# A hybrid attention and state-space layer: some inputs laid out by the host, and steps moved among groups, gates, turn and root

## The chip, the cores and the metric

The kernel runs on one core of a Trainium2 chip. The metric is the device time of one execution, in microseconds (us), as the median of several runs. The engines are named as in the profile: PE is TensorE (matmul; PEld is its weight load), DVE is VectorE, ACT is ScalarE, POOL is GpSimd, SP is SyncE, whose queue carries nearly all DMA issues of this kernel. PSUM is the memory that matmuls write; the kernel uses it in eight banks of 128 x 512 words.

## The reference, cut to what matters

One decoder layer with batch 1, sequence 1024 and model width 1024, all in fp32:

```python
c_act = silu(c)
shift, scale, gate = split(c_act @ w_ada + b_ada, 3)          # w_ada: 1024 x 3072
h = rms_norm(x, norm_in_gain) * (1 + scale) + shift
q, k, v, z_attn, xbc, dt_raw, z_ssm = split(h @ w_in)         # 4 x 1024, 1536, 16, 1024 columns
o = stick_breaking_attention(q, k, v)                         # 16 heads of 64
y_attn = rms_norm(o, sb_norm_gain) * silu(z_attn)
xs, B, C = split(silu(causal_depthwise_conv(xbc, conv_w, conv_b)))
dt = softplus(dt_raw + dt_bias); a = -exp(a_log)
y = ssd_scan(xs, dt, a, B, C, d_skip)                         # Mamba-2, 16 heads, chunks of 128
y_ssm = rms_norm(y * silu(z_ssm), ssm_norm_gain)
x = x + gate * (concat(y_attn, y_ssm) @ w_out)
out = rms_norm(x, norm_f_gain)
```

Stick-breaking attention weights key s for query t with sigmoid(z_ts) times the product of (1 - sigmoid(z_tj)) over the keys j between s and t.

## The kernel before

Projections run as fp32r matmuls of 512 columns in three terms: each operand is split into a high part (rounded to fp32r) and a low part (the rest), and high x high, low x high and high x low are summed in one PSUM bank. `hh[k]`, `hl[k]` are the two parts of the modulated and normalised x, features on partitions (k = 0..7, 128 features each) and 1024 tokens along the row; `whi`, `wlo` are those of a weight tile. A split costs a copy and a subtraction, on DVE and ACT.

The program has three stages. In the first and the third the order of every engine's instructions is that of the code (`pinned[0]` is true, and `K` or the `Engine` wrapper pins each instruction; that is why most DVE, ACT and SP instructions have line 62, the wrapper's, in the profile). In the second a scheduler orders them.

1. *Start.* `c` and other vectors are loaded as rows and turned into columns (`cols`) by a PE transpose (L125). x comes in eight tiles `xt[i]` of 128 tokens (named `big`), `w_ada`'s shift and scale columns in four quarters `c_` of 256 + 256 columns (`load_ada`, two DMAs for each of four tiles, rows of 1 KB). `norm_sq` squares a tile on ACT with a sum along the row, `norm_rt` makes the root on ACT and the reciprocal on DVE, `norm_by` scales the tile on DVE. `turn_x` transposes four 128 x 128 blocks on PE into a bank of `pt` or `pv` (L522); `h_full` modulates from there (scale `gsc`, shift `shc`) into `hh[k]` and a full copy (`hfs`, named `be`), and `h_low` subtracts for `hl[k]`. The first 512 tokens are `hb` = 0, the others `hb` = 1. `mm_h(k, hb)` is 12 matmuls (L562): the first four column tiles of `xbc`, summed over k in four `pz` banks. `fillers` (L582) are matmuls without a use of their own. After this `late_consts` makes columns of the convolution's and the norms' vectors, with two more transposes (L160, L163).
2. *State-space stage*, in the scheduler's order: the other `xbc` tiles, `dt`, the first values of attention, the convolutions, and two groups (`ssd_group`) of eight chunks, with gates (`gate_ssm`) and the first pair's q and k beside the second.
3. *Attention and output*, in the order of the code. Heads go in eight pairs p. `ROUND` lists a pair's steps: `scores` of a group of query blocks (L1028), `turned` (transposes of the weights and ACT's copies), `values` (L1120, into the one `pv` bank). Beside them run side jobs, a list for each pair (`SIDES`): gates, q and k, v, and at p = 6 the turn. `side_step` issues the next piece of a job, mostly three matmuls (L304 for features by tokens); `tick` moves a modelled clock, by which `after(t, f)` issues DMAs and splits later. A finished projection bank (`pj`, two of them) is emptied by ACT: the evacuations `evac` in `gate_ssm`, `qk` and `zgate` run a nonlinear pass (or the rounding copy) from the bank, then copy it to an `hf` tile with `emptied`, from which DVE goes on. `rows_s` is the root of the state-space output's sums of squares, within `inproj_v` (L350). `scores` has one rule on side work:

```python
        while side_left() and not 0.6 < left[0] < 3.6:
            side_step()
```

That is: before a group of scores the side job is moved to a place in a bank's sum where no evacuation is due (`left[0]` is what remains of it in us). `turn` is the last gate projection, with `hl` used up for good: it sums the terms with `hl` and `whi` first for both token halves, then loads `w_out`'s lower half into the freed `hl` tiles (`load_half`, tiles `wor`, one DMA for each 128 rows), and splits it while the other terms run. Then comes the output projection (`out_ssm`, L1163) and the tail with the final norm.

The profile's names: `pz`, `pj`, `pt`, `pv` are banks; `th`, `om`, `be`, `bc`, `bs`, `raw`, `st`, `sq`, `v`, `hf` are pools of tiles in SBUF. The functions that the change touches:

Of the kernel before, what the change touches and what calls it, by code (L numbers as in the profile page):

```python
# [26 lines left out]
def hybrid_layer_kernel(  # L27
# [3 lines left out]
    c: bass.AP,  # L31
    w_ada: bass.AP,
    b_ada: bass.AP,
    norm_in_gain: bass.AP,
    w_in: bass.AP,
    conv_w: bass.AP,
    conv_b: bass.AP,
    dt_bias: bass.AP,
    a_log: bass.AP,
    d_skip: bass.AP,  # L40
    sb_norm_gain: bass.AP,
    ssm_norm_gain: bass.AP,
# [81 lines left out]
    pr = bank(pv, "pv")  # L124
    K(T.transpose(pr[:, :32], rows[0:32, :], ident[0:32, 0:32]))  # L125
    cols = const("cols", [P, P])
    V.tensor_copy(cols[:, 0:32], pr[:, :32])
    cact = const("cact", [P, 8])
# [1419 lines left out]
```

## Time and profile before

| what | value |
|---|---|
| time, median of 3 runs | 1049.31 us (1048.99 to 1051.03) |
| time of the profiled execution | 1048.86 us |
| its span | 1047.1 us |
| PE busy | 1031.9 us, 99% |
| DVE busy | 766.5 us, 73% |
| ACT busy | 547.8 us, 52% |
| granted TensorE clock, mean | 0.999 |
| DMA | 96.17 MB, mean 92 GB/s |

The span runs from the first to the last instruction that the profiler recorded. A PE record of a matmul is longer than the distance to the next one, since matmuls are pipelined, so a PE that shows 99% can still have room within its instructions; the distance from one start to the next is the measure of what a matmul costs. In the rows of groups and of the timeline the fields are start (in a timeline), duration, engine, line, operation, output <- inputs, shape, type and count; what stands in brackets is idle time of the engine just before, and what ended it. In the rows of windows the first number is the window's length, then come PE, PEld, DVE, ACT and POOL with their busy time and count, the granted clock, the DMA engines' busy share (in us) and GB/s.

### The profile page before, as it was taken

Reading aid. Unit: us, or ns where it says so; the run is one execution under the profiler, and the core shown is the slowest. Engines: PE = TensorE matmul, PEld = TensorE weight load, DVE = VectorE, ACT = ScalarE, POOL = GpSimd, SP = SyncE. Lnnn points to the kernel's source line nnn. Section 1 sums busy time; section 2 is a strip of 40 time slices with the busy share of each in tenths; the row PEclk is TensorE's granted clock in tenths of the full one; section 3 lists DMA queues with packets and bytes.
Section 4 is the critical chain, followed back from the end, with each engine's and each line's share of the span. In section 5 each row is a group of like instructions: output and inputs, shape, how many; then the busy total and the mean of one; then the engine's idle time right before and its main releaser. Section 6 shows DMA issues by size and latency. Waiting matters only on the chain.

```text
span 1047.1 us, 16416 instructions
## 1 busy us (share of the span) xinstructions
PE 1031.9 (99%) x6365; PEld 847.2 (81%) x6365; DVE 766.5 (73%) x1339; ACT 547.8 (52%) x1218; POOL 2.7 (0%) x23
## 2 busy tenths in 40 slices
PE   7999999999999999999999999999999999999997
PEld 5789888777888887898887888878977778788886
DVE  5738879998838884764897668987578879755554
ACT  4755497767415564564554556555457556521111
POOL 0000000000000000000000000000000000000000
PEclk9999999999999999999999999999999999999999
DMA  9610333233302221111221102311120522665432
GB/s 349 238 42 22 84 105 106 71 102 101 101 21 61 81 81 30 56 27 41 81 71 41 51 21 81 81 42 41 32 63 29 202 101 71 214 221 172 148 114 78
DMA packets 91562, 96.17 MB, mean 92 GB/s; under 512 B 5998, under 2 KB 75994, under 8 KB 91484
## 3 DMA queue, kind: packets, MB, share of 16 engines
q1 hardware_dynamic: 88828, 86.45, 26.1%
q10 hardware_dynamic: 2656, 8.67, 2.6%
q8 instruction: 50, 0.82, 0.3%
q14 instruction: 28, 0.23, 0.1%
HBM read 78.26 MB, written 16.84 MB: 91 GB/s over the span
## 4 chain that ended last, share of the span: by engine, by line
PE 93%; DVE 2%; ACT 2%; DMA 2%; issue 0%; SPq 0%; DVEq 0%; ACTq 0%
PE pj L304 40%; PE pj L1163 16%; PE pv L1120 6%; PE pt L1093 3%; PE pz L562 3%; PE pj L350 3%; PE pj L354 3%; PE pj L351 3%; PE pz L1093 3%; PE pj L1028 2%; PE pz L1028 2%; PE pt L1028 2%; PE pz L824 1%; PE pv L838 1%; PE pz L829 1%; PE pj L1497 1%
## 5 line engine op out<-in xcount | busy, mean ns | idle before, releaser
L304 PE MATMUL pj<-hh,whi 128*128 128x512 f32 x544 | 220.2, 405 | 0.0
L304 PE MATMUL pj<-hh,wlo 128*128 128x512 f32 x544 | 214.0, 393 | 0.0
L304 PE MATMUL pj<-hl,whi 128*128 128x512 f32 x544 | 212.5, 391 | 0.0
L304 PEld LDWEIGHTS pj<-hh,whi 128*128 128x128 f32 x544 | 102.2, 188 | 23.9 <-issue 5.5
L304 PEld LDWEIGHTS pj<-hh,wlo 128*128 128x128 f32 x544 | 102.1, 188 | 22.6 <-issue 0.7
L304 PEld LDWEIGHTS pj<-hl,whi 128*128 128x128 f32 x544 | 102.4, 188 | 19.9 <-issue 1.0
L62 DVE TENSOR_TENSOR wlo<-raw,whi 128x512 fp32r<-128x512 f32 (+1 forms) x109 | 75.3, 692 | 23.5 <-ACT whi L62 16.6
L62 DVE TENSOR_TENSOR_SCAN om<-om 128x896 f32<-128x896 f32 (+2 forms) x48 | 87.3, 1818 | 1.7
L62 ACT COPY be<-pt 128x512 f32<-128x512 f32 (+1 forms) x80 | 38.6, 503 | 64.6 <-PE pt L1093 63.9
L350 PE MATMUL pj<-whi,hh 128*128 128x256 f32 (+1 forms) x224 | 65.1, 291 | 0.5 <-ACT v L62 0.5
L354 PE MATMUL pj<-whi,hl 128*128 128x256 f32 (+1 forms) x224 | 64.4, 288 | 0.0
L351 PE MATMUL pj<-wlo,hh 128*128 128x256 f32 (+1 forms) x224 | 63.6, 284 | 0.0
L1028 PE MATMUL pz<-big,big 64*128 64x256 f32 (+2 forms) x432 | 59.7, 334 | 0.0
L62 DVE TENSOR_TENSOR be<-be,om 128x767 f32<-128x767 f32 (+2 forms) x64 | 56.9, 889 | 3.1 <-DVE be L62 0.4
L62 ACT ACTIVATE be<-pz 128x127 f32<-128x127 f32 (+4 forms) x112 | 58.6, 529 | 0.0
L62 DVE TENSOR_TENSOR_SCAN bc<-bc 128x128 f32<-128x128 f32 (+2 forms) x64 | 56.6, 885 | 2.2
L304 PE MATMUL pj<-hh,st 128*128 128x512 f32 x160 | 56.1, 400 | 0.0
L1120 PE MATMUL pv<-be,v 128*64 128x256 f32 (+1 forms) x512 | 53.7, 362 | 0.0
L62 ACT ACTIVATE be<-be,acum 128x128 f32<-128x128 f32 x128 | 39.5, 390 | 24.5 <-DMA be<-acT_d 19.3
L1120 PEld LDWEIGHTS pv<-be,v 128*64 128x64 f32 x512 | 34.8, 137 | 20.1 <-issue 4.7
L62 DVE CAST whi<-raw 128x512 fp32r<-128x512 f32 x75 | 31.3, 418 | 23.2 <-PE pj L354 16.0
L62 ACT ACTIVATE th<-v 128x1024 f32<-128x1024 f32 (+2 forms) x9 | 8.5, 944 | 73.7 <-DVE v L62 73.7
(301 smaller groups left out, 2321.0 us busy)
## 6 DMA issues: line engine op xcount, KB each, us to landing
raw<-in_w_in_dram SPq DMA_DIRECT2D x98, 256.0 KB, 2.8
be<-acT_d ACTq DMA_DIRECT2D x16, 512.0 KB, 4.0
big<-in_x_dram SPq DMA_DIRECT2D x10, 512.0 KB, 6.5
aw<-in_w_ada_dram SPq DMA_DIRECT2D x16, 256.0 KB, 5.8
u_d<-big SPq DMA_DIRECT2D x8, 512.0 KB, 2.6
y_d<-bc SPq DMA_DIRECT2D x8, 512.0 KB, 2.6
raw<-in_w_ada_dram SPq DMA_DIRECT2D x16, 256.0 KB, 2.6
raw<-u_d SPq DMA_DIRECT2D x16, 256.0 KB, 2.9
```

What stands on the lines that cost most here:

```text
L62: return lambda *args, **kw: K(op(*args, **kw))
L304: K(T.matmul(ps, w[:, ws], h[:, b * HALF:(b + 1) * HALF], start=(k == 0 and n == 0), stop=(k == KT - 1 and n == 2)))
L350: K(T.matmul(ps[:, :n], h_hi[k][:, ts_], whi[:, ws], start=(k == 0), stop=False))
L351: K(T.matmul(ps[:, :n], h_hi[k][:, ts_], wlo[:, ws], start=False, stop=False))
L354: K(T.matmul(ps[:, :n], h_lo[k][:, ts_], whi[:, ws], start=False, stop=(k == KT - 1)))
L562: K(T.matmul(acc[f][:, c0:c1], w[:, f * P:(f + 1) * P], h[:, sl], start=(k == 0 and n == 0 and c0 == 0), stop=(k == KT - 1 and n == 2)))
L824: K(T.matmul(po, xd[:, 0, h, :], m[:, h, :], start=True, stop=(ch == 0)))
L829: K(T.matmul(po, st[:, h, :], abc[:, h, :], start=False, stop=True))
L1028: K(T.matmul(zs[b, e][:, y0:y0 + mw], a[r, i * P:(i + 1) * P], k_[r, m0:m0 + mw], start=(n == 0), stop=(n == 2)))
L1093: K(T.transpose(from_[:, (j - j0) * P:(j - j0 + 1) * P], be[:, j * P:(j + 1) * P], ident))
L1120: K(T.matmul(ps[64 * e:64 * e + 64, (q0 + u) * P:(q0 + 2) * P], vs[p][:, j * P + 64 * e:j * P + 64 * e + 64], tl[e][:, u:2, x0 + j * P:x0 ...
L1163: K(T.matmul(ps, y[:, ks], w(k, b), start=(k == 0 and n == 0), stop=(k == KT - 1 and n == 2)))
```

## The change

*Inputs.* The host hands over, beside x as it is, `x_t` (the second 512 tokens of x with features first, eight tiles of 128 x 512), `w_mod` (`w_ada`'s shift and scale columns as four quarters of four tiles 128 x 1024 that lie in one piece), `w_gate` and `b_gate` (the gate's columns), and `vecs` (the vectors as 148 columns). The row loads, the three transposes and the copies behind them go; `cols` is loaded in two DMAs, 32 columns first and 116 late. `load_ada` is one DMA a tile, 4 KB rows. The tile `xt[4]` is loaded ahead of the last quarter of `w_ada`, and `xt[5]` to `xt[7]` alternate with the last two weight tiles; `x_t` comes behind them.

*Second half of x.* `xt[4]` to `xt[7]` are read for their sums of squares alone: tiles 4 to 6 on ACT earlier than before, tile 7 on DVE. `scales` makes the reciprocals and multiplies the identity by them (four diagonals in an `hf` tile); four fp32 matmuls of ones by diagonals, between the two halves of `mm_h(6, 0)`, spread 1/rms of 512 tokens over all partitions in the `pv` bank. `second(k)` multiplies `x_t[k]` by that row on DVE, from PSUM and in place, and modulates the product as before, both passes on ACT and from SBUF. The 32 transposes of this half are gone.

*Groups, gates, turn, root.* The rule on side work is now a function, `to_window`, that `values` calls too, for pairs 0 to 6, once the next pair's q and k exist. In the pinned stage the gates' and `qk`'s evacuations copy the bank first and run the pass from the copy. `turn` orders its first matmuls so that `hl[0]` to `hl[3]` are free before the last six of the sixteen, and loads each pair of `w_out`'s blocks by one DMA as a tile comes free. The square root and reciprocal of `rows_s` wait in `quiet` for the next `turned` step of query block 2.

```diff
-    rows = mk(sp, "cbm", [P, 2, P], bufs=2)[:, 0, :]
-    A.dma_start(rows[0:8, :], c.rearrange("o (k p) -> (o k) p", p=P))
-    A.dma_start(rows[8:24, :], b_ada[:, 0:2048].rearrange("o (k p) -> (o k) p", p=P))
-    A.dma_start(rows[24:32, :], norm_in_gain.rearrange("o (k p) -> (o k) p", p=P))
+    cols = const("cols", [P, 192])
+    A.dma_start(cols[:, 0:32], vecs[:, 0:32])
...
-    pr = bank(pv, "pv")
-    K(T.transpose(pr[:, :32], rows[0:32, :], ident[0:32, 0:32]))
-    V.tensor_copy(cols[:, 0:32], pr[:, :32])
...
-            for e in range(2):
-                SP.dma_start(t_[:, :, e, :],
-                             w_ada[0][2 * n * P:2 * (n + 1) * P, e * D + c_ * 256:e * D + (c_ + 1) * 256]
-                             .rearrange("(k p) f -> p k f", p=P))
+            SP.dma_start(t_, w_mod[c_, n])
...
+    load_x(4)
     load_ada(3)
-    load_w4(6), load_w4(7)
-    for i in range(4, TB):
-        load_x(i)
-    late_loads()
+    load_x(5), load_w4(6), load_x(6), load_w4(7), load_x(7)
...
+    def by_rstd(k):
+        V.tensor_tensor(x_turned[k], x_turned[k], scale_of["row"], op=ALU.mult)
+    def scales(is_):
+        if not scale_of:
+            scale_of["diag"] = mk(sp, "hf", [P, HALF], bufs=2)
+        V.reciprocal(rstd[:, is_[0]:is_[-1] + 1], rstd[:, is_[0]:is_[-1] + 1])
+        for i in is_:
+            V.tensor_scalar_mul(scale_of["diag"][:, (i - 4) * P:(i - 3) * P], ident, rstd[:, i:i + 1])
+    def second(k):
+        by_rstd(k)
+        modulate(k, 1, x_turned[k])
...
+    load_xt()
+    late_loads()
+    V.scalar_tensor_tensor(junk, xt[7], 1.0, xt[7], op0=ALU.mult, op1=ALU.mult, accum_out=ssq[:, 7:8])
+    scales((4, 5, 6))
+    h_full(6, 0, pts[0])
+    h_low(6, 0)
+    norm_root(7)
+    scales((7,))
+    h_full(7, 0, pts[1])
+    split_lo(7)
+    h_low(7, 0)
+    mm_h(6, 0, (0, 1))
+    scale_of["row"] = bank(pv, "pv")
+    for i in range(4):
+        K(T.matmul(scale_of["row"][:, i * P:(i + 1) * P], ones, scale_of["diag"][:, i * P:(i + 1) * P],
+                   start=True, stop=True))
+    mm_h(6, 0, (2, 3))
+    second(0)
     mm_h(7, 0, (0, 1))
-    modulate(0, 1, full_v=True)
-    norm_by(6, 256), norm_by(7, 256)
+    second(1)
     mm_h(7, 0, (2, 3))
...
     for k in range(1, KT):
         if k + 2 < KT:
-            modulate(k + 2, 1)
+            second(k + 2)
         mm_h(k, 1)
...
-            A.activation(zg, ps, AF.Sigmoid)
-            V.scalar_tensor_tensor(zg, zg, cols[:, 92 + p:93 + p], emptied(ps), op0=ALU.mult, op1=ALU.mult)
+            full = emptied(ps)
+            A.activation(zg, full, AF.Sigmoid)
+            V.scalar_tensor_tensor(zg, zg, cols[:, 92 + p:93 + p], full, op0=ALU.mult, op1=ALU.mult)
...
+    def to_window():
+        while side_left() and not 0.6 < left[0] < 3.6:
+            side_step()
...
     def values(p, i_):
         while side_left() and clock[0] < free_at[0]:
             side_step()
+        if p < 7:
+            while p + 1 not in box:
+                side_step()
+            to_window()
...
-        for g, b in ((0, 0), (1, 0), (0, 1), (1, 1)):
-            for q in range(4):
+        for b, qs in ((0, (0, 1, 2, 3, 4, 5)), (1, (0, 1, 2, 3)), (0, (6, 7)), (1, (4, 5, 6, 7))):
+            for q in qs:
...
+                if b and q < 4:
+                    load_pair(0, q, hp.tile([P, 2, HALF], F32, tag=f"hl{q}", name=f"wor{q}"))
...
-            if (g, b) == (0, 1):
-                load_half(0, lambda q: hp.tile([P, 2, HALF], F32, tag=f"hl{q}", name=f"wor{q}"))
...
-        A.activation(r, r, AF.Sqrt, scale=1.0 / D, bias=eps_t[:, 1:2])
-        V.reciprocal(r, r)
+        def factors():
+            A.activation(r, r, AF.Sqrt, scale=1.0 / D, bias=eps_t[:, 1:2])
+            V.reciprocal(r, r)
+        quiet.append(factors)
...
             elif what == "t":
+                if i == 2 and quiet:
+                    quiet.pop()()
                 turned(p + before, i)
```

Instructions move on several engines. On DVE, at the entry to the second half of x, there stood before (`big` are the x tiles, `rstd` the reciprocals, `be` <- `raw`,`sq` the low part of a weight tile):

```order
L62 RECIPROCAL rstd<-rstd 128x1 x2
L62 TENSOR_SCALAR big_182<-big_182,rstd 128x1024
L62 TENSOR_SCALAR big_184<-big_184,rstd 128x1024
L62 TENSOR_TENSOR be_427<-raw_180,sq_495 128x512
L62 TENSOR_TENSOR hl_528<-be_203,hh_527 128x512
L62 TENSOR_TENSOR hl_532<-be_203,hh_531 128x512
L62 RECIPROCAL rstd<-rstd 128x1 x2
L62 TENSOR_SCALAR big_186<-big_186,rstd 128x256
L62 TENSOR_SCALAR big_188<-big_188,rstd 128x256
L62 TENSOR_SCALAR be_203<-pv_574,gsc,shc 128x512
L62 TENSOR_TENSOR hl_264<-be_203,hh_263 128x512
```

and now, in the same place (`hf` are the diagonals, `bc` the tiles of `x_t`, `pv_533` the row of scales):

```order
L56 SCALAR_TENSOR_TENSOR om_506,cols<-big_164 128x1024
L56 RECIPROCAL rstd<-rstd 128x3
L56 TENSOR_SCALAR hf_508<-ident,rstd 128x128 x3
L56 TENSOR_TENSOR hl_514<-be_168,hh_513 128x512
L56 RECIPROCAL rstd<-rstd 128x1
L56 TENSOR_SCALAR hf_508<-ident,rstd 128x128
L56 TENSOR_TENSOR be_392<-raw_162,sq_466 128x512
L56 TENSOR_TENSOR hl_522<-be_168,hh_521 128x512
L56 TENSOR_TENSOR bc_493<-bc_493,pv_533 128x512
L56 TENSOR_TENSOR hl_229<-be_168,hh_228 128x512
L56 TENSOR_TENSOR bc_493<-bc_493,pv_533 128x512
L56 TENSOR_TENSOR hl_240<-be_168,hh_239 128x512
```

The scalings of whole x tiles have gone; the square of the last tile and the diagonals come in ahead of the first-half `hl` parts, and a product stands before each second-half `hl`.

On PE, in the attention stage, the end of one pair's values before (`v` are attention values, `pv` their bank; L304 is a side job, L1028 the next scores):

```order
L1120 MATMUL pv_4932<-be_4103,v_806 64x128
L1120 MATMUL pv_4932<-be_4104,v_806 64x128
L304 MATMUL pj_4923<-hh_390,whi_681_4792 128x512
L304 MATMUL pj_4923<-hl_391,whi_681_4792 128x512
L304 MATMUL pj_4923<-hh_390,wlo_682_4793 128x512
L1028 MATMUL pj_4962<-big_4275,big_4165 128x512
L1028 MATMUL pz_4965<-big_4275,big_4165 128x512
```

and now the start and the end of the same values (L271 is the side job's line now, L1138 that of values, L1041 that of scores):

```order
L271 MATMUL pj_4863<-hh_355,whi_675_4732 128x512
L271 MATMUL pj_4863<-hl_356,whi_675_4732 128x512
L271 MATMUL pj_4863<-hh_355,wlo_676_4733 128x512
L1138 MATMUL pv_4875<-be_4043,v_746 64x256
...
L1138 MATMUL pv_4875<-be_4043,v_746 64x128
L1138 MATMUL pv_4875<-be_4044,v_746 64x128
L1041 MATMUL pj_4902<-big_4215,big_4105 128x512
L1041 MATMUL pz_4905<-big_4215,big_4105 128x512
```

The three side matmuls moved from behind the values to ahead of them.

On SP's queue, at the turn, there stood before (`raw` <- `u_d` are blocks of the state-space output that come back from DRAM, `wor` are blocks of `w_out`):

```order
L62 DMA raw_8240<-u_d 128x4x128
L62 DMA raw_8288<-u_d 128x4x128
L62 DMA wor_8294<-in_w_out_dram 128x512 x2
L62 DMA wor_8297<-in_w_out_dram 128x512 x2
L62 DMA wor_8300<-in_w_out_dram 128x512 x2
L62 DMA wor_8303<-in_w_out_dram 128x512 x2
```

and now:

```order
L56 DMA raw_8180<-u_d 128x4x128
L56 DMA wor_8215<-in_w_out_dram 128x2x512
L56 DMA wor_8218<-in_w_out_dram 128x2x512
L56 DMA raw_8232<-u_d 128x4x128
L56 DMA wor_8235<-in_w_out_dram 128x2x512
L56 DMA wor_8238<-in_w_out_dram 128x2x512
```

Two of the `wor` loads moved ahead of a `raw` load, and two DMAs of 128 rows became one of 256.

More of the change, by code (lines that the diff above doesn't have):

```diff
@@ L30, in hybrid_layer_kernel @@
     x: bass.AP,
[L31 to L34, printed above, removed]
-    w_in: bass.AP,
[L36 to L42, printed above, removed]
+    x_t: bass.AP,
+    vecs: bass.AP,
+    w_mod: bass.AP,
+    w_gate: bass.AP,
+    b_gate: bass.AP,
+    w_in: bass.AP,
     w_out: bass.AP,
@@ L452, in hybrid_layer_kernel, with load_xt @@
     load_w4(4), load_w4(5)
+    load_x(4)
     load_ada(3)
-    load_w4(6), load_w4(7)
-    for i in range(4, TB):
-        load_x(i)
-    late_loads()
+    load_x(5), load_w4(6), load_x(6), load_w4(7), load_x(7)
+    x_turned = []
+    def load_xt():
+        for k in range(KT):
+            if k % 2 == 0:
+                both = mk(sp, "bc", [P, 2, HALF], bufs=4)
+                x_turned.extend((both[:, 0], both[:, 1]))
+            SP.dma_start(x_turned[k], x_t[k])
     A.activation(rstd[:, 0:1], eps_t[:, 0:1], AF.Sqrt)
@@ L1000, in hybrid_layer_kernel @@
     seq = {"made": 0, "scanned": [], "weights": set()}
+    def to_window():
+        while side_left() and not 0.6 < left[0] < 3.6:
+            side_step()
     def scores(p, g):
         qh, ql, kh, kl = box[p]
-        while side_left() and not 0.6 < left[0] < 3.6:
-            side_step()
+        to_window()
         flush("A", lambda: not late["A"])
@@ L1186, in turn, with load_pair @@
         raw = {}
-        def load_half(g, tile_):
-            for q in range(4):
-                t = tile_(q)
-                for u in range(2):
-                    raw[2 * q + u, g] = t[:, u]
-                    r0 = 1024 + (2 * q + u) * P
-                    SP.dma_start(t[:, u], w_out[0][r0:r0 + P, g * HALF:(g + 1) * HALF])
+        def load_pair(g, q, t):
+            r0 = 1024 + 2 * q * P
+            SP.dma_start(t, w_out[0][r0:r0 + 2 * P, g * HALF:(g + 1) * HALF].rearrange("(u p) f -> p u f", p=P))
+            for u in range(2):
+                raw[2 * q + u, g] = t[:, u]
         def split_w(k, g, lo_eng):
@@ L1211, in second @@
         def second():
-            load_half(1, lambda q: mk(sp, "big", [P, 2, HALF], bufs=8))
+            for q in range(4):
+                load_pair(1, q, mk(sp, "big", [P, 2, HALF], bufs=8))
             for k in range(KT):
@@ L1217, in turn @@
         hooks["second"] = second
-        for g, b in ((0, 0), (1, 0), (0, 1), (1, 1)):
-            for q in range(4):
-                K(T.matmul(pss[b], wts[g][0][:, q * P:(q + 1) * P], h_lo[4 * g + q][:, b * HALF:(b + 1) * HALF],
-                           start=(g == 0 and q == 0), stop=False))
+        for b, qs in ((0, (0, 1, 2, 3, 4, 5)), (1, (0, 1, 2, 3)), (0, (6, 7)), (1, (4, 5, 6, 7))):
+            for q in qs:
+                K(T.matmul(pss[b], wts[q // 4][0][:, q % 4 * P:(q % 4 + 1) * P], h_lo[q][:, b * HALF:(b + 1) * HALF],
+                           start=(q == 0), stop=False))
+                if b and q < 4:
+                    load_pair(0, q, hp.tile([P, 2, HALF], F32, tag=f"hl{q}", name=f"wor{q}"))
                 if q % 2:
@@ L1534 @@
     nc = _bacc.Bacc("TRN2", target_bir_lowering=False, num_devices=1, dynamic_dma_scratch_size=4096)
+    given = {name: _np.asarray(a) for name, a in inputs.items()}
+    laid = {name: given[name] for name in ("x", "w_in", "w_out", "norm_f_gain")}
+    laid["x_t"] = given["x"][0, HALF:].T.reshape(KT, P, HALF)
+    laid["w_mod"] = (given["w_ada"][0, :, :2 * D].reshape(4, 2, P, 2, 4, 256)
+                     .transpose(4, 0, 2, 1, 3, 5).reshape(4, 4, P, S))
+    laid["w_gate"], laid["b_gate"] = given["w_ada"][0, :, 2 * D:], given["b_ada"][:, 2 * D:]
+    by_features = [given["c"], given["b_ada"][:, :2 * D], given["norm_in_gain"], given["conv_w"], given["conv_b"],
+                   given["sb_norm_gain"], given["ssm_norm_gain"], _np.repeat(given["d_skip"], 64)]
+    on_all = [_np.broadcast_to(given[name], (P, 16)) for name in ("dt_bias", "a_log")]
+    laid["vecs"] = _np.concatenate([a.reshape(-1, P).T for a in by_features] + on_all, axis=1)
     arrays, args = {}, []
     for name in _INS:
[L1537 removed]
+        a = _np.ascontiguousarray(laid[name])
         arrays[f"in_{name}_dram"] = a
```

88 lines of the change are left out of this document (34 added, 54 removed).

## The prediction

> **What bounds the kernel now.** I read the page first, then PE's waits, then the timeline and windows at each place that the diff touches.
>
> ```profile
> PE 1031.9 (99%) x6365; PEld 847.2 (81%) x6365; DVE 766.5 (73%) x1339; ACT 547.8 (52%) x1218; POOL 2.7 (0%) x23
> ...
> PE 93%; DVE 2%; ACT 2%; DMA 2%; issue 0%; SPq 0%; DVEq 0%; ACTq 0%
> ```
>
> The first row is busy time by engine, the second the chain that ended last. TensorE is the bound throughout: 93% of the chain. So an edit pays in one of three ways: it takes instructions off PE, it spares PE a switch between kinds of matmul, or it ends a wait of PE. What it saves on DVE, ACT or a queue is hidden. PE waits rarely; of the six rows that the view names these are the four longest:
>
> ```profile
> PE pv L125 <- DMA cbm<-in_norm_in_gain_dram: 5.4, 1, 5.4
> PE pj L1163 <- ACT hf L62: 1.1, 1, 1.1
> PE pj L350 <- ACT v L62: 0.5, 1, 0.5
> PE pz L824 <- DVE v L62: 0.4, 1, 0.4
> ```
>
> Who waited for whom, us in total, times, longest. The first waits for the small vectors, the second stands at the turn, the third at the root, the fourth among the chunks of the state-space stage.
>
> **The start.**
>
> ```profile
> 5.63 2.93 PE L582 MATMUL pz<-ident 128*128 128x128 f32 x12
> 11.16 1.52 PE L483 MATMUL pj<-aw,st 128*32 128x512 f32 x8
> 12.83 1.06 ACT L62 ACTIVATE om<-big 128x1024 f32<-128x1024 f32 x1 [3.78 <-DMA big<-in_x_dram]
> 16.34 0.74 PE L562 MATMUL pz<-hh,whi 128*128 128x256 f32 x4
> ```
>
> ```profile
> 24.00:28.00 4.00, 3.84 (x28) 2.57 (x28) 2.35 (x8) 1.53 (x3) 0.00 (x0) 1.00 1.09 389
> 36.00:40.00 4.00, 4.00 (x22) 3.40 (x23) 3.74 (x6) 3.97 (x9) 0.00 (x0) 1.00 1.01 408
> 40.00:50.00 10.00, 9.79 (x50) 7.86 (x50) 5.64 (x16) 8.93 (x18) 0.64 (x5) 1.00 0.29 72
> ```
>
> The timeline (start, duration) shows ACT waiting 3.78 us for the second block of x, which lands at 12.8 behind the first quarter of `w_ada`; the norm that follows sets the first projection matmul at 16.34. In the windows the last column is GB/s: 389 while `w_ada` comes in rows of 1 KB, 408 while x comes in rows of 4 KB; the stream is over soon after 40. The 5.4 us for the vectors lie under this stream, so that vectors as columns (no transpose, no copy) gain nothing at the start. Rows of 4 KB save 2.10 MB/389 - 2.10 MB/408 = 0.25 us a quarter, 1.0 in all; only what comes before 16.34 counts in full. Between 0.25 and 1.0 I take **-0.4**, near the one quarter that precedes.
>
> **The second half of x.** For each of the 8 steps PE has 12 matmuls of 512 columns, and before them 4 transposes.
>
> ```profile
> 60.58:66.99 6.41, 6.41 (x36) 5.29 (x34) 2.84 (x4) 3.84 (x6) 0.00 (x0) 1.00 0.36 88
> 66.99:72.56 5.57, 5.57 (x27) 4.59 (x25) 0.82 (x2) 1.45 (x2) 0.00 (x0) 1.00 0.05 15
> ```
>
> ```profile
> 123.09 0.38 PE L760 MATMUL pt<-st,tri 128*128 128x128 f32 x2
> 123.31 0.39 PE L761 MATMUL pt<-st,st 128*128 128x128 f32 x2
> ```
>
> Both windows hold two steps; in the second the transposes are over. The cost of 4 is (6.41 - 5.57)/2 = 0.42, and the second window still has one switch in it: between 0.42 and 0.49 I take 0.45, 3.6 for the eight. In their place stand 4 plain fp32 matmuls that spread 1/rms over the partitions. The next rows are such: 123.31 - 123.09 = 0.22 each, so 0.9 (up to 1.2 with a switch on both sides). Net **-2.7**.
>
> Is PE fed fast enough? New on DVE is a product of 128x512 with one operand in PSUM, ahead of ACT's two passes; DVE subtracts after them and only then does the next product, so the three make a ring.
>
> ```profile
> 38.96 0.69 DVE L62 TENSOR_TENSOR th<-th,pj 128x512 f32<-128x512 f32 x1
> 41.52 0.16 DVE L62 SCALAR_TENSOR_TENSOR gsc<-gsc,cols 128x2 f32<-128x2 f32 x1
> 43.26 1.07 PE L562 MATMUL pz<-hh,sq 128*128 128x512 f32 x4
> 47.95 0.59 PE L522 MATMUL pv<-ident,big 128*128 128x128 f32 x2 [0.21 <-DVE big L62]
> 50.98 0.19 PEld L562 LDWEIGHTS pz<-hl,whi 128*128 128x128 f32 x1 [0.58 <-DVE hl L62]
> ...
> 64.19 0.77 ACT L62 ACTIVATE hh<-pv,shc,gsc 128x512 fp32r<-128x512 f32 x1
> 64.86 0.77 ACT L62 ACTIVATE be<-pv,shc,gsc 128x512 f32<-128x512 f32 x1
> 65.67 0.69 DVE L62 TENSOR_TENSOR hl<-be,hh 128x512 fp32r<-128x512 f32 x1 [0.62 <-ACT be L62]
> ...
> 1021.28 1.28 DVE L62 SCALAR_TENSOR_TENSOR v<-v,fs,v 128x1024 f32<-128x1024 f32 x1
> ```
>
> Product 0.69 (the row at 38.96 has its shape and a PSUM operand), ACT 1.44 (64.19 to 65.63), subtraction 0.69: 2.82 a step, against PE's 12 x 0.227 = 2.72 (0.227 from start to start: four take 0.91, 72.56 less 66.99 holds 24). It loses 0.1 a step and needs a lead. The entry, all 0.4 earlier than now: the scales are ready at 41.3, DVE squares x7 (priced by the last row, 1.28) to 42.6, makes a reciprocal and three diagonals to about 43.6, and `hl6` to 44.3. PE wants `hl6` after four matmuls, at 42.9 + 0.9 = 43.8: a new wait of 0.5. Then the scales are spread at 45.6, product 46.3, ACT 47.8, `hl0` 48.5; PE comes to it 18 matmuls and a switch later, at 50.2. The lead of 1.7 falls to 1.0 by the last step, so no wait. ACT's copies of the last two finished banks now stand behind `hh1` and cost PE some 0.25. New waits 0.75, old ones 0.21 + 0.58: **0**, bounds -0.8 and +1.5. The transposed x (2.1 MB) follows x7 and needs 5.1 us at 408 GB/s, so its first block is there by 43 and its last by 47, ahead of the products at 45.6 and 65; the late vectors queue behind it on SP and are wanted at 70.
>
> **The late vectors.** Two transposes between projection matmuls go.
>
> ```profile
> 75.82 0.23 PE L160 MATMUL pv<-ident,st 76*128 76x76 f32 x1
> ```
>
> 0.15 each with the switch, **-0.3** (0 to -0.5). DVE's first convolutions may start some us earlier; no PE row waits for them.
>
> **The groups.** At seven places PE goes from values straight to scores; the matmuls between them (three, once six, once a longer stretch) stand before the values.
>
> ```profile
> 505.28 3.25 PE L1120 MATMUL pv<-be,v 128*64 128x256 f32 x32
> 508.45 0.50 PE L304 MATMUL pj<-hh,whi 128*128 128x512 f32 x1
> 508.79 0.39 PE L304 MATMUL pj<-hl,whi 128*128 128x512 f32 x1
> 509.02 0.40 PE L304 MATMUL pj<-hh,wlo 128*128 128x512 f32 x1
> 509.35 0.50 PE L1028 MATMUL pj<-big,big 64*128 64x512 f32 x1
> ```
>
> From start to start the first of the three takes 0.34 and the last 0.33, the middle one 0.23: two switches of 0.1 that end. 7 x 0.21 = **-1.5**; 0 if values to scores costs both.
>
> **Gates, root and turn.**
>
> ```profile
> 459.72 1.28 ACT L62 ACT_TABLE_LOAD   x1
> 465.73 0.38 PE L350 MATMUL pj<-whi,hh 128*128 128x256 f32 x1 [0.48 <-ACT v L62]
> 487.37 0.60 ACT L62 ACTIVATE om<-pj 128x512 f32<-128x512 f32 x1 [0.29 <-PE pj L1028]
> ...
> 827.33 0.58 ACT L62 COPY hf<-pj 128x512 f32<-128x512 f32 x1
> 827.96 0.50 PE L1163 MATMUL pj<-woh,st 128*128 128x512 f32 x1 [1.12 <-ACT hf L62]
> ```
>
> The gates' copy comes ahead of the nonlinear pass and frees its bank one pass, 0.58, earlier. PE waits for such a bank only at the turn, so alone it is 0; the second bank covers it.
>
> The root takes two table loads of 1.28 to the end of a turning step, where ACT has nothing due. The one back to the sigmoids falls before 487.37, where ACT waits only 0.29: the scores' passes run about 1 us late, and the second bank covers that. The wait of 0.48 goes: **-0.5** (0 to -0.6). [...]
>
> At the turn the loads of `w_out` are asked for block by block, two of them ahead of a load that waits on SP; so ACT is done with their splits when the gate's first half ends, and the bank is free in time: **-1.0** of 1.12 (0 to -1.1).
>
> **Sum.** -0.4 - 2.7 + 0 - 0.3 - 1.5 - 0.5 - 1.0 = -6.4. The profiled execution took 1048.86 us (span 1047.1), so 1042.5; the median of the runs, 1049.31, stands 0.45 above it: **1042.9**.
>
> **The rivals.** *The ring is late.* The splits of the next weights stand in it on DVE and ACT for four steps. At a product's 0.69 on each engine, were they in line, these steps would take 4.2: 4 x 1.48 + 4 x 0.1 less the lead 1.7 = 4.6. Against it: in the order ACT's split lies where DVE subtracts, and DVE's where ACT works. 1047.5.
>
> *The state-space stage waits, and the kernel is slower.* DVE has no room there:
>
> ```profile
> 150.00:200.00 50.00, 50.00 (x342) 39.72 (x341) 49.00 (x82) 38.23 (x77) 0.30 (x3) 1.00 0.28 80
> ```
>
> 49 of 50 us, and the order in this stage is planned anew. One of 16 chunks waits 0.4 for DVE. If each did for 0.6, that is 9.6: 1052.5. It decides from 0.53 a chunk on, the gain of 6.4 and the bound of 2.1 over 16. Against it: DVE starts earlier by several us and has fewer instructions.
>
> *PE warms up later.* The filling matmuls no longer stand behind the vectors' wait, so they run some 4 us earlier and PE idles before the modulation. In the profile they start 2.93/12 = 0.24 apart, and the modulation's later pass of 1.52 is not at that pace. If it and the sums behind it ran at half the pace, 1.3 of it would not lie beside x: 1044.2. [...] The page's granted clock, 1.00 from the first slice on, does not show it.
>
> *The late moves do not pay.* The waits at root and turn and the switches come back elsewhere: the start and the second half alone, -3.4, 1045.9. *More comes of it:* DVE's early start takes the 0.4 away, the entry's waits vanish, the stream gives its full 1.0: 1040.9.
>
> **Chances.** Forecast 0.54, ring 0.09, slower 0.05, warm-up 0.09, late moves 0.12, more 0.11. The range 1040.0 to 1046.8 leaves out the slower case, most of the ring and the tails. Beyond 0.2% (2.1 us, about what a measurement of this kernel tells from no change): faster 0.86, same 0.09, slower 0.05.
>
> **What would show it.** Right: the last projection matmul of the second half some 3 us earlier, no transposes after 45, no `3 x L304` between values and scores, no PE row that waits for `hf` or `v`. Wrong: PE rows waiting for `hl` or `hh` step after step (ring), for DVE in the state-space stage, or a later first projection matmul.

## The result, and the profile after

The changed kernel takes 1040.6 us in the median, the kernel before 1049.3 (six runs each). The ratio is 0.9914 (interval 0.9901 to 0.9928): 8.7 us less. One of the six runs of the change took 4479.86 us, for a reason that the record does not show; the ratio leaves it out. The forecast was 1042.9 in a range of 1040.0 to 1046.8: inside the range, 2.3 above the time. Of its terms one was far off, the start.

The page of the changed kernel, busy time by engine and the chain that ended last:

```profile
PE 1027.8 (99%) x6338; PEld 845.0 (81%) x6338; DVE 767.3 (74%) x1339; ACT 553.9 (53%) x1218; POOL 2.7 (0%) x23
...
PE 88%; DMA 5%; DVE 4%; ACT 2%; issue 1%; SPq 0%; POOL 0%; ACTq 0%; POOLq 0%; DVEq 0%
```

TensorE is the bound as before. What PE waits for has changed; only the wait for `v` in the state-space stage (L831, before L824) was there before:

```profile
PE pj L457 <- DVE st L56: 1.6, 1, 1.6
PE pz L556 <- POOL ident masks.py:199: 1.4, 1, 1.4
PE pz L831 <- DVE v L56: 1.0, 1, 1.0
PE pt L1106 <- ACT sq L56: 0.3, 1, 0.3
PE pz L536 <- ACT be L56: 0.2, 1, 0.2
```

The wait for the vectors (5.4), the one at the turn (1.1) and the one at the root (0.5) are gone. The first two rows now lie under the loads of the start.

PE is busy all the way, so the starts of its matmuls say where the time went. From the timelines, of before and then of after, the first projection matmul, one of the first scores and the last matmul of all:

```profile
16.34 0.74 PE L562 MATMUL pz<-hh,whi 128*128 128x256 f32 x4
...
312.90 0.49 PE L1028 MATMUL pz<-big,big 64*128 64x512 f32 x1
...
1039.81 0.28 PE L1497 MATMUL pj<-be,wlo 128*128 128x256 f32 x1
```

```profile
14.41 0.73 PE L536 MATMUL pz<-hh,whi 128*128 128x256 f32 x4
...
308.44 0.49 PE L1041 MATMUL pz<-big,big 64*128 64x512 f32 x1
...
1032.41 0.28 PE L1524 MATMUL pj<-be,wlo 128*128 128x256 f32 x1
```

| stretch | predicted | measured |
|---|---|---|
| start, to the first projection matmul | -0.4 | -1.93 |
| from there to the first scores (second half of x, late vectors, state-space stage) | -3.0 | -2.53 |
| from there to the last matmul (groups, root, turn) | -3.0 | -2.94 |
| behind the last matmul, to the end of the span | 0 | -0.5 |
| span | -6.4 | -7.9 |

The last row but one is not the change's doing: the span ends 7.3 after the last matmul in the profile of before, and 6.8 to 7.0 after it in that of the change and of all twelve experiments, two of them with the tail of before. The profiled execution of the change (1040.96) also stands 0.36 above its median, where that of before stood 0.44 below: 7.9 + 0.36 + 0.44 = 8.7.

### The profile page after: what moved, and what is told of

Read it like the earlier page. It is cut to its first block, busy times and chain, and to the rows that moved or that the text cites. A ratio compares the mean times of both kernels' runs of the same rounds, so it can differ in the third digit from the quotient of the medians.

```text
span 1039.2 us, 16321 instructions
## 1 busy us (share of the span) xinstructions
PE 1027.8 (99%) x6338; PEld 845.0 (81%) x6338; DVE 767.3 (74%) x1339; ACT 553.9 (53%) x1218; POOL 2.7 (0%) x23
## 4 chain that ended last, share of the span: by engine, by line
PE 88%; DMA 5%; DVE 4%; ACT 2%; issue 1%; SPq 0%; POOL 0%; ACTq 0%; POOLq 0%; DVEq 0%
PE pj L271 38%; PE pj L1181 16%; PE pv L1138 6%; PE pt L1106 3%; PE pj L317 3%; PE pj L321 3%; PE pj L318 3%; PE pz L1106 3%; PE pz L536 2%; PE pj L1041 2%; PE pz L1041 2%; PE pt L1041 2%; DVE big L56 2%; DMA aw<-in_w_mod_dram 1%; PE pz L831 1%; PE pj L1524 1%
## 5 line engine op out<-in xcount | busy, mean ns | idle before, releaser
L271 PE MATMUL pj<-hh,whi 128*128 128x512 f32 x544 | 220.0, 404 | 0.0
L271 PE MATMUL pj<-hh,wlo 128*128 128x512 f32 x544 | 213.8, 393 | 0.0
L271 PE MATMUL pj<-hl,whi 128*128 128x512 f32 x544 | 212.4, 390 | 0.0
L271 PEld LDWEIGHTS pj<-hh,whi 128*128 128x128 f32 x544 | 102.3, 188 | 23.3 <-issue 4.4
L271 PEld LDWEIGHTS pj<-hh,wlo 128*128 128x128 f32 x544 | 102.1, 188 | 22.8 <-issue 0.7
L271 PEld LDWEIGHTS pj<-hl,whi 128*128 128x128 f32 x544 | 102.4, 188 | 20.0 <-issue 1.0
L317 PE MATMUL pj<-whi,hh 128*128 128x256 f32 (+1 forms) x224 | 64.9, 291 | 0.0
L1041 PE MATMUL pz<-big,big 64*128 64x256 f32 (+2 forms) x432 | 59.7, 334 | 0.0
L56 ACT ACTIVATE be<-pz 128x127 f32<-128x127 f32 (+4 forms) x112 | 56.1, 502 | 0.0
L271 PE MATMUL pj<-hh,st 128*128 128x512 f32 x160 | 55.9, 399 | 0.0
L56 ACT COPY hf<-pj 128x512 f32<-128x512 f32 x52 | 32.0, 615 | 43.7 <-PE pj L271 42.9
L1138 PE MATMUL pv<-be,v 128*64 128x256 f32 (+1 forms) x512 | 53.7, 362 | 0.0
L1138 PEld LDWEIGHTS pv<-be,v 128*64 128x64 f32 x512 | 34.8, 137 | 20.1 <-issue 3.9
```

What stands on the lines that cost most here:

```text
L56: return lambda *args, **kw: K(op(*args, **kw))
L271: K(T.matmul(ps, w[:, ws], h[:, b * HALF:(b + 1) * HALF], start=(k == 0 and n == 0), stop=(k == KT - 1 and n == 2)))
L317: K(T.matmul(ps[:, :n], h_hi[k][:, ts_], whi[:, ws], start=(k == 0), stop=False))
L1041: K(T.matmul(zs[b, e][:, y0:y0 + mw], a[r, i * P:(i + 1) * P], k_[r, m0:m0 + mw], start=(n == 0), stop=(n == 2)))
L1138: K(T.matmul(ps[64 * e:64 * e + 64, (q0 + u) * P:(q0 + 2) * P], vs[p][:, j * P + 64 * e:j * P + 64 * e + 64], tl[e][:, u:2, x0 + j * P:x0 ...
```

## The experiments

A label with b_ is the kernel before with one part of the change added, one with a_ the changed kernel with one part undone or altered. Changes of one or two us are read from PE's starts in the profiles. Up to the first projection matmul these agree to 0.3 (14.27 to 14.58 in the seven kernels that have the changed start), and from one group of scores to the next to 0.02. Two places are less steady: the wait for `v` in the state-space stage, as the text says below, and the stretch with the turn, which varies by 0.5 where the program is the same.

### What made the start

*The modulation columns alone* (before, with `w_mod`):

```diff
-            for e in range(2):
-                SP.dma_start(t_[:, :, e, :], w_ada[0][2 * n * P:2 * (n + 1) * P, e * D + c_ * 256:...]...)
+            SP.dma_start(t_, w_mod[c_, n])
```

> The kernel before, with w_ada's shift and scale columns alone as the changed kernel has them (one DMA a tile, rows of 4 KB). Theory: these rows are the whole gain of the start, since the stream runs at about 415 GB/s instead of about 350 while the second block of x is waited for: first projection matmul at 14.4 to 14.8 instead of 16.34, time 1.5 to 1.9 less. Rival, the prediction's term: 15.9, time 0.4 less. Rival, the early vectors make the start: 16.3, time the same.

*The vectors alone* (before, with `vecs`):

```diff
-    A.dma_start(rows[0:8, :], c...), A.dma_start(rows[8:24, :], b_ada...), A.dma_start(rows[24:32, :], norm_in_gain...)
-    K(T.transpose(pr[:, :32], rows[0:32, :], ident[0:32, 0:32]))
+    A.dma_start(cols[:, 0:32], vecs[:, 0:32])
```

> The kernel before, with the vectors alone as columns (no row loads, no three transposes). Theory: PE's first matmul comes 4 us earlier and the first projection matmul stays at 16.3, give or take 0.2; only the two late transposes count, time 0.3 less. Rival, the vectors make the start: first projection matmul at 14.4 to 15, time 1.5 to 2 less.

Medians of ten runs each: 1048.46 and 1048.75, against 1049.08 of before, run beside them (ratios 0.9997, 0.9988 to 1.0007, and 0.9994, 0.9985 to 1.0004). Neither has the gain of the start by itself. With the columns alone the first projection matmul came at 15.21 (-1.13), where none of the three expectations had it; 0.5 of this was gone by the first scores, and 0.6 went into a longer wait at the turn (1.8 against 1.1). With the vectors alone it came at 16.91 (+0.57) in the profiled execution; with both, -1.93. The reason is that two paths meet there: the norm of the second block of x, and the modulation's sums. ACT's square of the second block, and DVE's scale of the modulation that is ready last, in the kernel with the columns alone:

```profile
10.66 1.06 ACT L63 ACTIVATE om<-big 128x1024 f32<-128x1024 f32 x1 [1.04 <-DMA big<-in_x_dram]
...
14.32 0.16 DVE L63 SCALAR_TENSOR_TENSOR gsc<-gsc,cols 128x2 f32<-128x2 f32 x1
```

and in the changed kernel:

```profile
10.84 1.06 ACT L56 ACTIVATE om<-big 128x1024 f32<-128x1024 f32 x1 [3.00 <-DMA big<-in_x_dram]
...
12.76 1.06 ACT L56 ACTIVATE om<-big 128x1024 f32<-128x1024 f32 x1 [0.44 <-DMA big<-in_x_dram]
...
13.07 0.16 DVE L56 SCALAR_TENSOR_TENSOR gsc<-gsc,cols 128x2 f32<-128x2 f32 x1
...
13.81 0.55 ACT L56 ACTIVATE hh<-pv,shc,gsc 128x256 fp32r<-128x256 f32 x1
```

The block lands at the same time, but without early vectors the modulation is 1.25 later and sets the start. In the changed kernel a third path is the last to end: ACT squares the third block of x (12.76) ahead of `hh`, and is done with it about half a us after the scale. With the vectors alone the block is the later path again, and in the profiled execution something comes on top: the windows of that kernel, with the granted clock behind POOL's column, and two rows of the modulation's matmuls.

```profile
3.00:6.00 3.00, 1.35 (x7) 1.05 (x5) 0.78 (x4) 1.24 (x2) 0.00 (x0) 1.00 1.01 357
6.00:9.00 3.00, 1.30 (x6) 0.39 (x8) 0.92 (x2) 1.79 (x5) 0.00 (x0) 0.82 1.06 350
9.00:12.00 3.00, 3.00 (x10) 0.70 (x10) 0.00 (x0) 0.00 (x0) 0.00 (x0) 0.50 1.07 414
12.00:15.00 3.00, 3.00 (x17) 1.66 (x10) 1.45 (x4) 1.90 (x4) 0.00 (x0) 0.54 1.02 409
```

```profile
6.64 1.05 PE L446 MATMUL pj<-aw,st 128*32 128x512 f32 x4 [2.29 <-DMA aw<-in_w_ada_dram]
8.75 1.92 PE L446 MATMUL pj<-aw,st 128*32 128x512 f32 x4 [1.06 <-DMA aw<-in_w_ada_dram]
```

PE had finished its filling matmuls early and stood still for 2.29 and 1.06 us. Its clock is 0.82, 0.50 and 0.54 in the last three windows: taken as either full or half, it was half for some seven us (1.1, 3.0 and 2.8, an estimate from these three), and four matmuls take 1.92 in place of 1.05. What sets the half clock off is not shown. The clock's column does not tell everything, though: it is 1.00 in the first us of every kernel here, but the fillers do not run at one pace. In the changed kernel, the first twelve and the last eight:

```profile
1.41 2.93 PE L556 MATMUL pz<-ident 128*128 128x128 f32 x12 [1.41 <-POOL ident masks.py:199]
...
13.23 1.06 PE L556 MATMUL pz<-ident 128*128 128x128 f32 x8
```

That is 0.24 and 0.13 each, and it is the same in before (2.93 for twelve at 5.63, 1.06 for eight at 15.22). So the prediction's third rival was right about the fillers, in every kernel. What it feared, the modulation's later pass at the slow pace, is in this execution (2.19 for eight at 11.22) and not in the changed kernel (1.41 at 9.25). That the vectors brought it is not shown. The execution took 1050.39 us with a mean granted clock of 0.995, while the other nine of this kernel have 0.997 to 0.999; two of before's nineteen (1050.92 and 1051.11) have 0.996. At the full pace this kernel would start near 16.2, as an estimate: ACT is done with the third block at 15.60 (14.54 + 1.06), and `hh` and the first projection matmul are 0.6 apart in the changed kernel. That is neither gain nor loss.

*Length of the rows, and number of DMAs.* Three kernels keep the changed kernel and alter how the modulation columns come: rows of 1 KB with one DMA a tile; rows of 4 KB with two DMAs of 64 partitions; rows of 1 KB with two DMAs of 128 partitions, packed.

```diff
-            SP.dma_start(t_, w_mod[c_, n])
+a_w1k       SP.dma_start(t_.rearrange("p (j f) -> p j f", f=256), w_mod[c_, n].rearrange("j p f -> p j f"))
+a_two       SP.dma_start(t_[:64, :], w_mod[c_, n][:64, :]); SP.dma_start(t_[64:, :], w_mod[c_, n][64:, :])
+a_w1k2      for e in range(2): SP.dma_start(<half e of t_>, w_mod[c_, n, e].rearrange("k p f -> p k f"))
```

> The changed kernel, with the modulation columns stored so that each DMA still brings a whole tile, but in rows of 1 KB. Theory, it is the length of the rows: stream near 350 to 390 GB/s, first projection matmul at 15.3 to 16.3 instead of 14.41. Rival, it is the number of DMAs that SP has to issue: 14.4, unchanged.

> The changed kernel, with rows of 4 KB but two DMAs a tile (64 partitions each), so that SP issues as many as before. Theory, the length of the rows: first projection matmul at 14.4 to 14.6. Rival, the number of issues: SP is done with the first quarter at about 6 us instead of 3, and the matmul comes at 15.5 to 16.3.

> The changed kernel with the modulation columns packed in rows of 1 KB and two DMAs a tile, each over all 128 partitions, so that SP issues as many and as long rows as before. Theory, the number of DMAs ahead of the second block of x is the larger part: its square starts at 12.2 to 12.8 (12.63 with the vectors alone, 11.24 with one DMA a tile). Rival, it is the distance of the rows in the old array of 12 KB: 11.2, as with one DMA a tile.

| modulation columns | SP asks for the second block of x at | its square starts | MB moved by then | first projection matmul |
|---|---|---|---|---|
| 4 KB, one DMA (the change) | 3.14 | 10.84 | 3.44 | 14.41 |
| 1 KB, one DMA | 3.38 | 11.24 | 3.37 | 14.83 |
| 1 KB, two DMAs, packed | 5.75 | 11.94 | 3.55 | 15.50 |
| 1 KB, two DMAs, in `w_ada` (vectors alone) | 5.83 | 12.63 | 3.81 | 16.91 |
| the same, vectors as rows (before) | 6.33 | 12.83 | 3.95 | 16.34 |

Of the 2.0 us by which the block comes earlier, the rows' length is 0.4, the number of DMAs 0.7, the place in the old array 0.7, and the vectors' own loads 0.2, taken in this order and from one profile each. The seven kernels with the changed start have the square at 10.69 to 10.99, so that the 0.2 is no more than the spread, and the 0.4 little more. Both theories of these runs had one cause too few, and the expectation for the last kernel (12.2 to 12.8) was missed in the middle between theory and rival.

The MB (GB/s of the window from 0 to the square, times its length) tell a slower stream from one that brings other bytes first; the block and what was asked for ahead of it are 3.15 MB in each kernel. With eight DMAs in place of four, 0.18 MB more had moved when the block was there, 0.4 us at 414 GB/s (the changed kernel's mean from 3 to 9), and the stream was slower from 3 to 6 (335 against 375 GB/s). With the rows in the old array it was 0.26 MB more, 0.6 us. So these two parts are for the most part bytes of later loads that come ahead of the block; why they do stays open.

Rows of 1 KB cost something behind the start too: the kernel with one DMA took 1042.12 and the packed one 1043.35 (one run each), and in the first PE spends 0.8 more in the sums of the third quarter and 0.3 more where it waits for `hl6`.

The kernel with 64 partitions a DMA does not tell rows from DMAs, because it has a cost of its own:

```profile
6.00:10.00 4.00, 2.64 (x6) 0.43 (x8) 0.92 (x2) 1.86 (x5) 0.00 (x0) 1.00 1.05 246
10.00:14.00 4.00, 3.42 (x12) 0.65 (x10) 0.00 (x0) 0.00 (x0) 0.00 (x0) 1.00 1.01 271
```

The stream falls to 246 and 271 GB/s, the first projection matmul comes at 18.17, later than theory and rival had it, and the time rises to 1057.61 (one run).

*Does the block hold the start, or are both paths level?* The second block is loaded ahead of the last tile of the first quarter:

```diff
-    load_ada(0)
-    load_x(1)
+    load_ada(0, lambda: load_x(1))      # called ahead of the fourth tile
```

> The changed kernel with the second block of x loaded ahead of the fourth tile of the first quarter of the modulation columns. Theory, the norm of this block and the modulation now end level, so that an earlier block gains nothing: its square starts near 9.6, the modulation's sums come 0.6 to 1.2 later, first projection matmul at 14.4 to 15.0, time the same within 0.6. Rival, the block alone holds the start: first projection matmul at 13.2 to 13.8, time 0.6 to 1.2 less.

```profile
9.50 1.06 ACT L56 ACTIVATE om<-big 128x1024 f32<-128x1024 f32 x1 [1.72 <-DMA big<-in_x_dram]
...
14.03 0.16 DVE L56 SCALAR_TENSOR_TENSOR gsc<-gsc,cols 128x2 f32<-128x2 f32 x1
```

The block came 1.3 earlier, the modulation 0.96 later, the first projection matmul 0.51 later (14.92); 1041.02 in the median of four runs. Level, as the theory had it. But the third block of x has as many bytes ahead of it as in the changed kernel and lands no earlier (its square at 12.67 against 12.76), so this kernel does not show what an earlier second block is worth when the third is earlier too.

### The second half of x

*Undone* (x tiles scaled and transposed as before, loads in the new order):

```diff
-    load_xt()
...
-    scales((4, 5, 6)) ... second(0) ... second(k + 2)
+    norm_by(4), norm_by(5) ... modulate(0, 1, full_v=True) ... modulate(k + 2, 1)
```

> The changed kernel with the second half of x as before: x tiles scaled on DVE and transposed on PE, no x_t, no row of scales. Theory: 32 transposes come back and 4 fp32 matmuls go, so that the time from the first projection matmul to the first scores is 2.6 to 3.2 longer, nothing else. Rival, the new ring on DVE and ACT ate part of the gain: under 2 longer.

1045.46 in the median of five runs, 4.9 over the change; the stretch from the first projection matmul to the first scores is 4.45 longer. Of this the transposes are +3.57 and the row of scales -0.81, so 2.8 as expected. Some 1.6 more are waits among the projection matmuls at the entry, the longest of them

```profile
42.62 1.20 PE L536 MATMUL pz<-hh,sq 128*128 128x512 f32 x4 [0.77 <-ACT hh L56]
```

where ACT squares two blocks of x ahead of `hh6`, after it has waited 0.73 and 1.32 for the last two weight tiles to land, which now alternate with x's blocks. "Nothing else" was wrong: the old entry has these squares on ACT between the weights' landing and `hh6`, and the new one has moved them. Behind the entry a wait of 1.2 for `st` comes and the one for `v` goes, with little left over.

*The ring.* In the changed kernel DVE's product, ACT's passes and DVE's subtraction, and what PE does meanwhile:

```profile
53.04 0.68 DVE L56 TENSOR_TENSOR bc<-bc,pv 128x512 f32<-128x512 f32 x1
...
53.75 0.82 ACT L56 ACTIVATE hh<-bc,shc,gsc 128x512 fp32r<-128x512 f32 x1 [0.82 <-DVE bc L56]
...
54.48 0.80 ACT L56 ACTIVATE be<-bc,shc,gsc 128x512 f32<-128x512 f32 x1
...
55.31 0.69 DVE L56 TENSOR_TENSOR hl<-be,hh 128x512 fp32r<-128x512 f32 x1 [0.95 <-ACT be L56]
55.92 0.68 DVE L56 TENSOR_TENSOR bc<-bc,pv 128x512 f32<-128x512 f32 x1
56.06 0.42 PE L317 MATMUL pj<-whi,hh 128*128 128x272 f32 x2
```

55.92 - 53.04 = 2.88 a step, and it is 2.88 in every step; the forecast had 2.82. PE does not wait: the scheduler has put matmuls of the first value projection (L317) between the pinned ones. Whether that cover was needed:

```diff
-                K(T.matmul(ps[:, :n], h_hi[k][:, ts_], whi[:, ws], start=(k == 0), stop=False))
+                first = T.matmul(ps[:, :n], h_hi[k][:, ts_], whi[:, ws], start=(k == 0), stop=False)
+                tc.keep_in_program_order(first) if with_dt and k == 0 else K(first)
```

> The changed kernel, with the first matmul of each token tile of the first value projection kept behind the second half of x, so that the scheduler can't put them between its steps. Theory, the steps' ring (2.88 us a step against 2.72 on PE) starts with a lead and PE needs no cover: the last projection matmul of the second half comes at 70.5 instead of 74.4, and the first scores within 0.3 of 308.4. Rival, the value matmuls covered a ring that was late: PE waits for hl or hh among the steps, and the first scores come 1 to 4 us later.

The last projection matmul came at 71.14, the first scores 0.14 later than in the changed kernel, 1041.3 in the median of four runs. Without the cover PE waits once near the end of the ring, and once more in the value projection:

```profile
PE pj L317 <- ACT st L56: 0.6, 1, 0.6
PE pz L537 <- DVE hl L56: 0.5, 1, 0.5
```

So PE waits half a us at the ring's end, not 4.6, and the schedule gives it back in other places (the wait of L831 for `v` is gone in this kernel). The theory held but for that half. And the half is not the ring's own pace: its products come 2.88 to 2.91 apart here too, but for one step of 4.20, where ACT's split of a weight tile stands ahead of `hh` and waits for its load:

```profile
57.41 0.65 ACT L56 CAST whi<-raw 128x544 fp32r<-128x544 f32 x1 [1.59 <-DMA raw<-in_w_in_dram]
```

Without that wait the last `hl` would be done at 67.5, as in the changed kernel (66.83 + 0.69), and PE asks for it at 68.3: a lead of 0.8, as an estimate.

### Groups, turn, root, gates

```diff
a_nogroups, in values:
-        if p < 7:
-            while p + 1 not in box:
-                side_step()
-            to_window()
```

> The changed kernel without the new step in values: side matmuls stand between values and scores again. Theory: seven times two switches come back, 0.2 each: 1.4 more between the first scores and the turn. Rival, PE pays two switches in either place: 0.

```diff
a_noturn, in turn:
-        for b, qs in ((0, (0, 1, 2, 3, 4, 5)), (1, (0, 1, 2, 3)), (0, (6, 7)), (1, (4, 5, 6, 7))):
-                    load_pair(0, q, ...)
+        for g, b in ((0, 0), (1, 0), (0, 1), (1, 1)):
+                load_half(0, ...)           # after (0, 1), one DMA for each 128 rows
```

> The changed kernel with the turn as before (order of its matmuls, one DMA for each 128 rows of w_out, asked for together). Theory: PE waits 1.1 for hf at the output projection again: 1.0 to 1.2 more. Rival, the gates' early copies had ended that wait already: under 0.3 more.

```diff
a_noroot, in rows_s:
-        quiet.append(factors)
+        A.activation(r, r, AF.Sqrt, ...); V.reciprocal(r, r)
```

> The changed kernel with the root of the state-space output's norm where it was, between two scores. Theory: PE waits again behind the two table loads, 0.5 to 0.75 more between the second and third pair's scores. Rival, the early copies have made room and the wait stays away: 0.

```diff
a_nogates, in the evacuations of gates, q and k:
-            full = emptied(ps)
-            A.activation(zg, full, AF.Sigmoid)
+            A.activation(zg, ps, AF.Sigmoid)
+            full = emptied(ps)
```

> The changed kernel with the pass from the bank ahead of the copy again in the gates and in q and k. Theory: 0, no bank is waited for there, and PE's distances stay the same to 0.1 in the attention stage. Rival, the copies are what ended the wait at the turn: 0.5 to 1.1 more there.

*Groups:* 1.33 more from the first scores to the last matmul, in steps of 0.2 at the seven places; 1042.27 (one run). In the changed kernel the values now follow the side matmuls and the scores follow the values:

```profile
500.25 0.39 PE L271 MATMUL pj<-hh,wlo 128*128 128x512 f32 x1
500.57 3.25 PE L1138 MATMUL pv<-be,v 128*64 128x256 f32 x32
503.75 0.50 PE L1041 MATMUL pj<-big,big 64*128 64x512 f32 x1
```

The switch into the values (0.32 from the last side matmul) stayed; the values take 3.18 to the scores, as they took 3.17 to the side matmuls before.

*Turn:* 1.3 more between the turn's first matmul and the output projection; 1043.09 (one run). The wait is back, by the waits of that kernel, with the gates' copies in place. It was 1.1 in before, and 1.8 and 1.6 with the columns and the vectors alone, so that its worth is known to some 0.7 only:

```profile
PE pj L1181 <- ACT hf L56: 1.3, 1, 1.3
```

*Root:* 0.74 more between the sixth and the seventh group of scores; 1041.80 (one run). The wait of before is back:

```profile
PE pj L317 <- ACT v L56: 0.5, 1, 0.5
```

In the changed kernel the table loads stand here, in a turning step and at the next pass:

```profile
471.24 1.28 ACT L56 ACT_TABLE_LOAD   x1
472.54 0.30 ACT L56 ACTIVATE r_s<-r_s,eps_t 128x8 f32<-128x8 f32 x1
...
481.70 1.28 ACT L56 ACT_TABLE_LOAD   x1
```

Each is followed by its pass 0.02 after its end (at 472.54 and 483.00).

*Gates:* 1040.87 in the median of four runs against 1040.6 of the changed kernel, run at another time, and 0.02 of difference at the last matmul if the wait in the state-space stage, which comes ahead of the altered lines, is set aside. The copies cost a wait of 0.3 in one place (`pt` for `sq`, in the list above) and save one of 0.3 at the turn (for `be`, in this kernel's list), the latter within what that stretch varies by. Nothing in sum, as expected.

That wait in the state-space stage, L831 for `v`, was 0.4 in the profile of before and 1.0 in that of after. It was 0.8 with the modulation columns alone, where PE, DVE and ACT run before's program word for word, and 1.0, 1.4 and 0.4 with groups, turn and gates undone, whose programs are the changed one's up to there. It varies by itself, by about half a us either way.

## Why the prediction was right, and where it was not

*Start: the term was mis-sized, -0.4 against -1.93.* The step that failed is the price of the earlier rows: it took the rates of streams in full flow (389 and 408 GB/s) and one quarter's bytes, 0.25, and said that the vectors gain nothing. The stream that is waited for is another one: in the windows of before the stream of the first quarter carries

```profile
3.00:6.00 3.00, 0.58 (x2) 0.55 (x3) 0.19 (x1) 0.50 (x2) 0.00 (x0) 1.00 1.01 352
6.00:9.00 3.00, 3.00 (x16) 2.57 (x19) 0.78 (x4) 2.94 (x6) 0.00 (x0) 1.00 1.04 363
```

and in those of after

```profile
3.00:6.00 3.00, 1.39 (x9) 1.13 (x9) 0.78 (x4) 1.23 (x2) 0.00 (x0) 1.00 1.03 406
6.00:9.00 3.00, 3.00 (x9) 0.45 (x10) 0.92 (x2) 1.79 (x5) 0.00 (x0) 1.00 1.03 421
```

But the rate is the smaller part. From the span's start to the square in the changed kernel, and to the square in before, before moved

```profile
0.00:10.84 10.84, 5.42 (x22) 3.30 (x23) 1.89 (x7) 4.31 (x7) 1.21 (x10) 1.00 0.83 289
0.00:12.83 12.83, 7.41 (x32) 3.99 (x33) 1.99 (x8) 4.31 (x8) 1.21 (x10) 1.00 0.86 308
```

and after

```profile
0.00:10.84 10.84, 7.82 (x32) 3.78 (x33) 1.83 (x7) 4.31 (x8) 1.21 (x10) 1.00 0.82 317
```

So at 10.84 before was 0.30 MB behind, 0.7 us at 414 GB/s, the mean of 406 and 421. Then it moved on to 3.95 MB before its block was there, where the changed kernel had needed 3.44: 0.51 MB, or 1.2 of the 2.0 us, are bytes of other loads that came ahead of the block. The prediction's term has no such part. And the vectors were not for nothing: they are worth 0.8 (15.21 to 14.41) once the block comes early, because the modulation is the second path, and nothing alone. The prediction also took the second block's norm for the last step of before's start; `hh` starts there at 15.74, when ACT is done with the square of the third block (14.68 + 1.06).

*Second half of x: right in its parts.* Transposes -3.43 with the wait among them (forecast -3.6), the four fp32 matmuls +0.81 (0.9). The new waits at the entry stayed at 0.2 where 0.75 was forecast: everything ran 1.8 earlier than before, and ACT's passes followed at once. The sum of the stretch came to -2.53 and not -3.0 because PE's modulation matmuls took 0.35 more and the wait for `v`, which varies by itself, 0.5 more. Two of the signs were not met as they were written: the last projection matmul came 1.2 earlier (75.59 to 74.42) and not 3, since some 30 matmuls of the value projection stand ahead of it where before had 4, and the row that waits for `v` is still there.

*The ring rival (1047.5)* had the right rate (2.88, even above the forecast). No split lengthens a step in the changed kernel; in the one without the cover one did, which made a step of 4.20 and a wait of 0.5 at the end. The forecast's "no wait" rested on a lead of 1.0 at the last step, which the estimate of 0.8 bears out, and in the changed kernel on a cover that it had not seen in the order: the scheduler may put work that is free to move between pinned instructions.

*The slower rival (1052.5)* asked for 0.53 a chunk; one chunk waited, 1.0 in all. *More comes of it (1040.9)* stands nearest to the time, and not for its reasons alone: the entry's waits did all but vanish, and the start gave more than the full 1.0, but by the order of the loads and the vectors, and DVE's wait of 0.4 grew instead of going.

*Late vectors, groups, root, turn:* -0.3, -1.5, -0.5, -1.0 forecast. In the trace the two late transposes held 0.2, the groups are seven steps of 0.21 to 0.22; the root gave 0.72 and the turn 0.96 (in the stretch that varies by 0.5), and undoing them brought back 1.33, 0.74 and 1.3. The price of the table loads held: they take 1.28 each in the changed kernel too, the pass follows 0.02 later, and the wait did not come back.

*The sum* was off by 2.3: 1.5 at the start, 0.5 behind the last matmul and 0.8 from how the two profiled executions stand to their medians, less 0.5 between. The middle two, 1.3, come from which executions were profiled and are no fault of the working.

## What to carry to other kernels

Where a kernel starts on its loads, read the rate in the window that is waited for and not in the stream's middle (352 and 363 GB/s here, not 389 and 408), compare the bytes moved by the time a load is there with those that were asked for ahead of it, and list every path that meets at the first big matmul: an edit to one of two level paths can pay little or nothing and both together pay (here 1049.08 became 1048.46 and 1048.75 by either alone, and the start 1.93 less by both). Where TensorE is busy throughout, price an edit by start-to-start distances of its matmuls; instructions taken out, switches and end-waits priced so came out within 0.3 each here. A ring that is a little slower than PE (here 2.88 a step against 2.72) needs a lead, and here it had one to its end; what stood in line in it and waited 1.59 for a load made a step of 4.20.

## What was not expected of the hardware

- A DMA of 64 partitions in rows of 4 KB, in turns with one on the other 64, moved 246 to 312 GB/s, in the windows from 6 to 34, where the change's DMAs of 128 partitions moved 416 to 420: 17 us in all for 16 tiles (1057.61 against 1040.6). Why is not shown.
- TensorE's matmuls run at half the pace in the first us of every kernel here, though the column of the granted clock says 1.00: twelve fillers take 2.93 us (0.24 each), eight later ones 1.06 (0.13). When the full pace comes differs from profile to profile: with the changed start, two kernels (groups undone, second half undone) have it at 5.80 and 5.88 (1.05 for four of the modulation's matmuls) and keep it over a pause of 0.2, the other five take 2.97 to 3.38 for the first eight, in place of the 2.1 that twice 1.05 would be. In one execution, with the vectors alone, it was there at 6.64 (1.05 for four) and fell back to half (1.92 for four at 8.75, a clock of 0.50 from 9 to 12) for some seven us, after pauses of 2.29 and 1.06 with 1.05 of work between.
